# A key norm's reciprocal square root on two engines: square root and reciprocal, or logarithm and exponential

## The chip, the cores and the metric

The kernel runs on one core of a Trainium2 chip. The metric is the time of one execution on the device in microseconds (us), as the median of several runs. Beside the plain runs there is one profiled execution, from which a hardware trace tells what each engine did and when: TensorE (PE, its matmuls, and PEld, its loads of weights), VectorE (DVE), ScalarE (ACT), GpSimd (POOL), SyncE (SP, which issues most transfers), and the DMA engines.

## What is computed

One inference step of a backbone with a single layer, for 512 latent tokens and 128 context tokens, 640 in all, 2,048 channels wide, all in fp32. A layer is an RMS norm with modulation, an input projection `w_in`, a mixer, an output projection, and a gated feed-forward network. Half of the mixer is a bidirectional linear recurrence with 16 heads of 64 channels (RWKV-7), the other half a gMLP with 8 groups. The part that matters here is how the keys of the recurrence are normalised, head by head:

```
kk = heads(k * lp['k_k'])
kk = kk * lax.rsqrt(jnp.maximum(jnp.sum(kk * kk, axis=-1, keepdims=True), 1e-24))
...
y, s_fin = _delta_scan(rh, decay, kd, vh, -kk, kk * heads(a), s0[:, d], reverse=(d == 1))
```

So every key vector of 64 channels is divided by its length. The factor is one number for each token and head, the reciprocal square root of a sum of squares.

## The kernel before

All 640 tokens are held at once, with channels on the 128 partitions and tokens along the free dimension. A projection's 128 output channels for all tokens are a block of 128x640, made as two halves of 320. Since the weights are fp32 and the matmuls take a shorter form of it, each weight piece is split into a high part (ACT, line 172) and a rest (DVE, line 173), and each product is made of three matmuls (lines 194, 195 and 198).

The program has three long stages: the input projection with everything that the mixer needs of each block; the recurrence, with the output projection beside it; and the feed-forward network. The change lies in the first stage.

That stage goes over 43 blocks of `w_in` (list `blocks`, lines 969 to 982). Each block costs 32 small steps of matmuls, which the kernel counts in `wide[0]`; four pieces of 512 input channels make a block, and the split of a piece is issued two pieces ahead (`LEAD`). When a block is complete, `take` (line 996) copies it from PSUM and hands it to a generator that does the rest of its work: `take_r` for a pair of heads' receptance, `take_v` for its values, `take_k` for its keys, `take_gv` and `take_gu` for a gMLP group. The recurrence has eight pairs of heads, and for each pair the order is r, v, k, with one gMLP group or several behind some pairs.

`take_k` (line 562) is by far the longest. For one pair it smooths the keys (lines 572 and 477), squares them and sums the squares over each head with a matmul by a block matrix of ones (`head_sums`, line 519, matmuls at lines 530 and 531), makes the factor (lines 582 to 589), multiplies the keys by it to the tile `nkk` (line 590), and from there makes decay rates (`rates`, matmuls at 605 and 606, tanh at 609; `decays`, line 612), the rows `R` and `X` for the chunk matrices (`rows`, line 629), and the chunk matrices themselves (`chunks`, line 667, matmul at line 677, masked by DVE at lines 688 and 689), for the forward and the backward scan. In its wake come `solve` (line 832), a long chain of small DVE operations (lines 848 and 850), and `merge` (line 862).

How this work is mixed with the projection's matmuls is planned by hand. Every generator yields now and then a number, its estimate of what it has just issued, in a unit of roughly a microsecond; a `Mixer` runs generators until a budget of such units is used up. For the block work the budget comes from a pace: each block has a cost (2.6 for r, 5.1 for v, `KCOST` for k, 12.0 and 5.0 for a gMLP group) and a due time, three blocks ahead:

```python
mixA.add(blocks[b][1](pr), blocks[b][2], wide[0] + 32 * RAW)      # line 1002, RAW = 3
...
for cost, end in self.ends:                                        # line 423, pace()
    need += max(0.0, cost)
    most = max(most, need / max(1, end - wide[0]))
...
mixA.run(f * max(AMIN, 8.0 * mixA.pace()))                         # line 1007, f = 1/4
```

Line 1007 runs four times in each piece of 8 steps, so that one step hands out about as many units as the pace says. `mixS` runs `solve` and `mixM` runs `merge` beside it. The tile framework then puts the instructions of each engine into an order, which need not be that of the program text; in this stage only `in_turn` fixes an order by hand.

On ACT the functions come out of tables, and the trace shows an instruction ACT_TABLE_LOAD where the next function needs another one. In the profile before there are two for each pair: one charged to line 584 (the square root) and one to line 609 (the next tanh).

Of the kernel before, what the change touches and what calls it, by code (L numbers as in the profile page):

```python
# [13 lines left out]
AF = mybir.ActivationFunctionType  # L14
# [10 lines left out]
HALF = T // 2  # L25
# [35 lines left out]
REST = 6  # L61
LATE = 2
OFF = 13
KCOST = 50.0
GORD = (1, 1, 2, 2, 3, 4, 4, 8)
KAP = math.exp(-0.5)
GC0 = math.sqrt(2.0 / math.pi)
# [22 lines left out]
def flow_step(ctx: ExitStack, tc, x_prompt, x_sample, state_rwkv, c, c_ctx, w_mod, b_mod,  # L90
# [4 lines left out]
    V, S, G, TE = nc.vector, nc.scalar, nc.gpsimd, nc.tensor  # L95
# [27 lines left out]
    for h in range(2):  # L123
        s = slice(CH * h, CH * h + CH)
# [9 lines left out]
    for h in range(2):  # L134
        s = slice(CH * h, CH * h + CH)
# [76 lines left out]
    with ExitStack() as ph:  # L212
# [133 lines left out]
        for j in range(4):  # L346
# [5 lines left out]
            for kb in range(4 * j, 4 * j + 4):  # L352
                hf = p0b.tile([P, T], F32, name="hf")
# [208 lines left out]
    def take_k(pr, p):  # L562
# [18 lines left out]
        ssq = bp.tile([P, T], F32, tag="t2", name="ssq", bufs=1)  # L581
        yield from head_sums(sq, lambda ps, s: V.tensor_scalar_max(ssq[:, s], ps, 1e-24))
        yield 1.0
        S.activation(ssq, ssq, AF.Sqrt)
        yield 0.5
        for hf in range(2):
            s = slice(HALF * hf, HALF * hf + HALF)
            V.reciprocal(ssq[:, s], ssq[:, s])
            yield 2.0
        V.scalar_tensor_tensor(out=nkk, in0=nkk, scalar=-1.0, in1=ssq, op0=ALU.mult, op1=ALU.mult)  # L590
        fs = bk.tile([P, T], F32, tag="fs", name="fs", bufs=1)
        yield 0.8
# [378 lines left out]
    def block(col, fn, cost, i):  # L971
        blocks.append((col, lambda pr: fn(pr, i), cost))

    g = 0
    for p in range(NPAIR):
        block(P * p, take_r, 2.6, p)
        block(2 * DA + P * p, take_v, 5.1, p)
        block(DA + P * p, take_k, KCOST, p)
        while g < GORD[p]:
            block(CSH + DA + P * g, take_gv, 12.0, g)  # L980
            block(CSH + P * g, take_gu, 5.0, g)
            g += 1
# [489 lines left out]
    with ExitStack() as ph:  # L1472
# [58 lines left out]
        for hf in range(2):  # L1531
            s = slice(HALF * hf, HALF * hf + HALF)
# [638 lines left out]
```

## Time and profile before

The table gives what matters; stage borders are read from the first and last start of the lines named.

| what | value |
|---|---|
| median of three runs | 3188.06 us (3185.64, 3188.06, 3188.2) |
| profiled execution, its own time | 3182.42 us |
| span of that execution's trace | 3180.6 us |
| mean granted TensorE clock in it | 0.993 of full speed |
| input projection's matmuls (line 194), first and last start | 49.5 and 1062.0 us |
| square root (line 584), first and last start | 195.1 and 901.3 us |
| reciprocal (line 588), first and last start | 195.8 and 905.4 us |
| product with the keys (line 590), first and last start | 200.3 and 907.6 us |

"Busy" is the time in which an engine had an instruction in work; the records of matmuls overlap, since they are pipelined. "Idle before" is the time in which an engine stood still ahead of an instruction, and the name behind `<-` is what ended that wait. A "window" view gives the busy time of each engine in stretches of the span, with the number of instructions in brackets, the granted clock as a share of full speed, and the share of the DMA engines.

### The profile page before, as it was taken

To read this page: it belongs to the slowest core of one execution; us is meant where nothing else is said; L and a number is where in the kernel's file an instruction comes from. 1 tells how busy PE (TensorE), PEld (TensorE's weight loads), DVE (VectorE), ACT (ScalarE), POOL (GpSimd) and SP (SyncE) were. 2 spreads that over 40 slices of the span, in tenths; PEclk is the share of its full clock that TensorE was granted. 3 is DMA by queue.
4 is the path that set the end of the run, shared out by engine and by line. 5 is a ranking of instruction groups with operands and counts; after the bars stand their busy time and mean duration, and the time that the engine had idled before them with its cause. 6 is when DMAs were issued, how large, how long until landed. Compare 5 with 4: busy or idle time off the path is not lost.

```text
span 3180.6 us, 71623 instructions
## 1 busy us (share of the span) xinstructions
PE 3059.6 (96%) x27896; PEld 2844.7 (89%) x27896; DVE 2354.6 (74%) x4119; ACT 1474.4 (46%) x3216; POOL 1238.2 (39%) x1081
## 2 busy tenths in 40 slices
PE   6999999999999999999999999999999999999997
PEld 3788878788878888899999999999999999999997
DVE  4567777667776688767977777777777787888888
ACT  3344544544454444357544444444444454444365
POOL 2001121221122034411456665666656645555542
PEclk9999999999999999999999999999999999999999
DMA  9767786867777688575343434434343364554453
GB/s 371 249 190 201 213 233 175 218 196 203 210 208 202 205 285 275 157 221 155 110 132 107 121 118 127 122 107 127 119 122 119 109 200 150 159 167 123 135 163 123
DMA packets 740436, 550.84 MB, mean 173 GB/s; under 512 B 141056, under 2 KB 673504, under 8 KB 731264
## 3 DMA queue, kind: packets, MB, share of 16 engines
q1 hardware_dynamic: 727136, 532.47, 55.4%
q0 software_dynamic: 10624, 13.23, 1.8%
q8 instruction: 219, 3.59, 0.5%
q14 instruction: 121, 0.99, 0.1%
q10 hardware_dynamic: 2336, 0.57, 0.1%
HBM read 437.79 MB, written 110.95 MB: 173 GB/s over the span
## 4 chain that ended last, share of the span: by engine, by line
PE 45%; DVE 3%; issue 1%; DMA 1%; POOL 1%; ACT 0%; SPq 0%; DVEq 0%; POOLq 0%; ACTq 0%
PE P L1688 15%; PE P L1685 15%; PE P L1686 15%; DVE lo L1466 1%; DMA opd<-d_op 0%; DVE xd L1754 0%; DMA x1d<-d_x 0%; POOL rawd L1594 0%; DVE cd L1944 0%; DMA rawd<-in_w_ffn_down_dram 0%; DVE out L2138 0%; DVE acc L1925 0%; ACT hi L1465 0%; DMA xd<-d_os 0%; POOL t L1594 0%
## 5 line engine op out<-in xcount | busy, mean ns | idle before, releaser
L1685 PE MATMUL P<-xo,hi 128*128 128x320 f32 x2352 | 699.3, 309 | 0.2 <-ACT hi L1465 0.2
L1686 PE MATMUL P<-xo,hi 128*128 128x320 f32 x2352 | 699.1, 309 | 0.0
L1466 DVE TENSOR_TENSOR lo<-raw,hi 128x512 fp32r<-128x512 f32 x526 | 513.0, 981 | 162.3 <-ACT hi L1465 159.8
L1465 ACT CAST hi<-raw 128x512 fp32r<-128x512 f32 x526 | 326.9, 622 | 466.4 <-PE P L1686 384.2
L1688 PE MATMUL P<-xo,lo 128*128 128x320 f32 x2352 | 440.8, 309 | 5.0 <-DVE lo L1466 5.0
L194 PE MATMUL big<-h_hi,hi 128*128 128x320 f32 x1376 | 438.4, 325 | 6.8 <-ACT hi L172 3.9
L1685 PEld LDWEIGHTS P<-xo,hi 128*128 128x128 f32 x2352 | 441.3, 188 | 0.5 <-ACT hi L1465 0.5
L1686 PEld LDWEIGHTS P<-xo,hi 128*128 128x128 f32 x2352 | 441.6, 188 | 0.0
L195 PE MATMUL big<-h_lo,hi 128*128 128x320 f32 x1376 | 423.1, 314 | 0.8 <-DVE h_lo L358 0.7
L1594 POOL TENSOR_TENSOR raw<-raw 128x512 f32<-128x512 f32 x252 | 410.2, 1637 | 10.1 <-DVE lo L1466 1.8
L1688 PEld LDWEIGHTS P<-xo,lo 128*128 128x128 f32 x2352 | 369.0, 188 | 6.0 <-DVE lo L1466 6.0
L1685 PE MATMUL P<-xd,hi 128*128 128x320 f32 x1232 | 367.7, 310 | 5.5 <-ACT hi L1465 2.3
L1686 PE MATMUL P<-xd,hi 128*128 128x320 f32 x1232 | 366.8, 309 | 0.0
L198 PE MATMUL big<-h_hi,lo 128*128 128x320 f32 x1376 | 320.1, 313 | 2.1 <-DVE lo L173 2.1
L194 PEld LDWEIGHTS big<-h_hi,hi 128*128 128x128 f32 x1376 | 261.9, 190 | 57.2 <-issue 25.3
L173 DVE TENSOR_TENSOR lo<-raw,hi 128x512 fp32r<-128x512 f32 x268 | 185.2, 694 | 156.1 <-ACT hi L172 154.4
L1594 POOL TENSOR_TENSOR t<-raw 128x512 f32<-128x512 f32 x84 | 125.1, 1490 | 425.3 <-DMA raw<-in_w_ffn_up_dram 362.0
L1465 ACT CAST hi<-rawd 128x512 fp32r<-128x512 f32 (+1 forms) x288 | 167.0, 585 | 225.3 <-PE P L1686 153.3
L172 ACT CAST hi<-raw 128x512 fp32r<-128x512 f32 x268 | 164.5, 618 | 223.2 <-PE big L195 86.1
L195 PEld LDWEIGHTS big<-h_lo,hi 128*128 128x128 f32 x1376 | 262.0, 190 | 5.8 <-DVE h_lo L358 1.9
L1466 DVE TENSOR_TENSOR lo<-rawd,hi 128x512 fp32r<-128x512 f32 (+1 forms) x288 | 241.3, 844 | 24.6 <-ACT hi L1465 24.3
L1688 PE MATMUL P<-xd,lo 128*128 128x320 f32 x1232 | 236.9, 310 | 7.2 <-DVE lo L1466 7.2
(406 smaller groups left out, 6085.4 us busy)
## 6 DMA issues: line engine op xcount, KB each, us to landing
wt<-in_w_mod_dram SPq DMA_DIRECT2D x96, 1024.0 KB
raw<-in_w_ffn_gate_dram SPq DMA_DIRECT2D x182, 256.0 KB
raw<-in_w_ffn_up_dram SPq DMA_DIRECT2D x182, 256.0 KB
rec<-d_S SPq DMA_DIRECT2D x80, 576.0 KB
raw<-in_w_in_dram SPq DMA_DIRECT2D x172, 256.0 KB
rawd<-in_w_ffn_down_dram SPq DMA_DIRECT2D x128, 256.0 KB
raw<-in_w_out_dram SPq DMA_DIRECT2D x96, 256.0 KB
xd<-d_os SPq DMA_DIRECT2D x66, 320.0 KB
```

What stands on the lines that cost most here:

```text
L172: S.copy(hi, raw)
L173: V.tensor_sub(lo, raw, hi.bitcast(F32))
L194: TE.matmul(halves[hf], hi[:, k, :], h_hi[:, kb, s], start=(kb == 0), stop=False)
L195: TE.matmul(halves[hf], hi[:, k, :], h_lo[:, kb, s], start=False, stop=False)
L198: TE.matmul(halves[hf], lo[:, j - 4 * q, :], h_hi[:, j, s], start=False, stop=(j == KB - 1))
L1465: S.copy(hi[:, 0:nk], raw[:, 0:nk])
L1466: V.tensor_sub(lo[:, 0:nk], raw[:, 0:nk], hi[:, 0:nk].bitcast(F32))
L1594: G.tensor_tensor(out=o[:, 0:nk], in0=p[:, 0:nk], in1=q[:, 0:nk], op=ALU.subtract)
L1685: TE.matmul(ps, hi[:, k, :], xk[:, 0, :], start=q == 0 and k == 0 and not filled, stop=False)
L1686: TE.matmul(ps, hi[:, k, :], xk[:, 1, :], start=False, stop=False)
L1688: TE.matmul(ps, lo[:, k, :], x(i, 4 * q + k)[:, 0, :], start=False, stop=q == nq - 1 and k == nk - 1 and last)
```

## The change

The square root on ACT and the two reciprocals on DVE, each over one half of the tile, are replaced by two ACT operations over the whole tile: the natural logarithm, and an exponential that is given the scale -0.5. Both compute `ssq ** -0.5`. The yields behind them are changed: 0.5, 2.0 and 2.0 go, and one of 1.0 comes. The cost of a key block in the planner goes down by the same 3.5.

```diff
-KCOST = 50.0
+KCOST = 46.5
...
         yield from head_sums(sq, lambda ps, s: V.tensor_scalar_max(ssq[:, s], ps, 1e-24))
         yield 1.0
-        S.activation(ssq, ssq, AF.Sqrt)
-        yield 0.5
-        for hf in range(2):
-            s = slice(HALF * hf, HALF * hf + HALF)
-            V.reciprocal(ssq[:, s], ssq[:, s])
-            yield 2.0
+        S.activation(ssq, ssq, AF.Ln)
+        S.activation(ssq, ssq, AF.Exp, scale=-0.5)
+        yield 1.0
         V.scalar_tensor_tensor(out=nkk, in0=nkk, scalar=-1.0, in1=ssq, op0=ALU.mult, op1=ALU.mult)
```

## The prediction

> **What bounds the kernel now.** I read the page's summary first, then a table of windows, then the waits of TensorE, and last the groups of the lines that change.
>
> ```profile
> span 3180.6 us, 71623 instructions
> PE 3059.6 (96%) x27896; PEld 2844.7 (89%) x27896; DVE 2354.6 (74%) x4119; ACT 1474.4 (46%) x3216; POOL 1238.2 (39%) x1081
> ```
>
> Over the span TensorE is the bound: it stands still for only 3180.6 - 3059.6 = 121.0 us. What VectorE is spared is worth nothing by itself; it pays only where PE waits for it. So I look at the stretch of 30 us that begins with each of the eight pairs' first reciprocal (the starts come from the timeline of line 588), and at what lies between those stretches.
>
> ```profile
> 195.80:225.80 30.00, 29.16 (x216) 24.18 (x214) 26.82 (x41) 17.11 (x38) 4.32 (x8) 1.00 0.58 160
> 299.10:329.10 30.00, 25.80 (x295) 22.23 (x294) 26.61 (x38) 14.02 (x28) 0.53 (x1) 1.00 0.31 82
> 384.70:414.70 30.00, 27.73 (x194) 23.52 (x193) 29.62 (x67) 15.08 (x32) 1.17 (x2) 1.00 0.61 178
> 500.30:530.30 30.00, 30.00 (x282) 25.14 (x281) 28.47 (x43) 15.23 (x33) 1.55 (x3) 1.00 0.60 170
> 595.20:625.20 30.00, 28.15 (x203) 24.42 (x202) 29.51 (x69) 15.27 (x32) 2.26 (x4) 1.00 0.60 181
> 703.90:733.90 30.00, 28.68 (x211) 25.48 (x210) 27.39 (x41) 15.21 (x32) 2.12 (x4) 1.00 0.54 147
> 817.80:847.80 30.00, 26.24 (x387) 22.68 (x387) 27.34 (x42) 14.92 (x30) 0.00 (x0) 1.00 0.59 167
> 902.10:932.10 30.00, 26.20 (x183) 23.30 (x182) 28.77 (x66) 13.97 (x29) 0.40 (x1) 0.94 0.55 169
> sum 240.00, PE 221.95 PEld 190.95 DVE 224.54 ACT 120.83 POOL 12.35; mean PE 27.74 PEld 23.87 DVE 28.07 ACT 15.10 POOL 1.54
> ```
>
> ```profile
> sum 576.20, PE 561.34 PEld 475.76 DVE 351.75 ACT 284.01 POOL 142.29; mean PE 70.17 PEld 59.47 DVE 43.97 ACT 35.50 POOL 17.79
> ```
>
> The columns are busy times of PE, PEld, DVE, ACT and POOL, then the granted clock, the DMA share and GB/s; the last row is the sum over the eight stretches in between, up to 1012 us. Behind each reciprocal DVE is busy 28.07 of 30 us (94%), and PE idles 240.00 - 221.95 = 18.05 us. In between DVE is busy 351.75 of 576.20 us (61%), and PE idles only 14.86 us in more than twice the time. So the first 30 us behind the norm are the place where DVE, and not PE, sets the pace, and the reciprocals stand at its head. ACT is half idle there. Whom PE waits for in the stage (180 to 960 us) agrees:
>
> ```profile
> PE pG L677 <- DVE GA L689: 8.1, 8, 2.4
> PE pG L677 <- DVE mix L848: 3.8, 1, 3.8
> PE pwa L605 <- ACT tha L609: 2.7, 4, 1.3
> PE ptm L180 <- issue: 2.6, 1, 2.6
> ```
>
> (Total us, times, longest.) The largest waits are for DVE's masking of the chunk matrices, a dozen DVE operations behind `nkk`. The tanh, the third, waits in part for DVE as well, whose reads free its tile.
>
> **The change, part by part.** The rows of what goes, what comes, and what has to serve as a price:
>
> ```profile
> L588 DVE RECIPROCAL ssq<-ssq 128x320 f32<-128x320 f32 x16 | 33.7, 2131 | 9.1 <-ACT ssq L584 9.1
> L584 ACT ACTIVATE ssq<-ssq 128x640 f32<-128x640 f32 x8 | 5.9, 740 | 6.0 <-DVE ssq L582 6.0
> L625 ACT ACTIVATE L<-L 128x640 f32<-128x640 f32 x16 | 11.8, 738 | 0.4
> L584 ACT ACT_TABLE_LOAD x8 | 10.3, 1283 | 0.1
> L609 ACT ACT_TABLE_LOAD x8 | 10.3, 1283 | 1.7 <-PE pwa L606 1.6
> ```
>
> *Removed from DVE:* two reciprocals for each pair, 2 x 2.131 = 4.26 us, over eight pairs 34.1 us. They are in no transfer and on no queue but DVE's.
>
> *Exchanged on ACT:* a square root of 0.740 us for a logarithm, and an exponential more. An exponential of this shape takes 0.738 us (line 625). The logarithm is in no row; since the square root and the exponential differ by 2 ns, I take 0.74. ACT gets 8 x 0.74 = 5.9 us more. Queued behind the two are the casts of the weight pieces (line 172) and the copies out of PSUM; ACT is busy 15.10 of 30 us here, and that idle half hides the addition, so I price it at nothing. Without the cover it would be 5.9 us.
>
> *Table loads:* two for each pair now, one for the square root, and one back for the tanh. The exponential of line 625 has none: it shares a table with the tanh. So if the logarithm's table holds no exponential, the load back merely moves from the tanh to the exponential. I take the same two. The bounds are a third load (logarithm, exponential and tanh all apart), 8 x 1.283 = 10.3 us more on ACT, and none at all, 20.5 us less; neither is on the bounding engine while ACT has its idle half. The Trainium skill, "ScalarE: Activation LUTs", section "What ACT_TABLE_LOAD costs", puts a change of tables at about 2.66 us, since a drain of 1.38 us comes ahead of the load. The rows show 0.1 us of idle ahead of all eight loads of line 584 together, so no such drain; by that price the third load would cost ACT an estimated 21.3 us, and my sum would stay as it is, because ACT does not set it.
>
> *The chain from the sum of squares to `nkk`:* square root plus two reciprocals, 0.74 + 4.26 = 5.00 us, become 2 x 0.74 = 1.48 us, 3.52 us shorter (2.24 with a third load in the way).
>
> *The planner.* The yields between the sum and `nkk` fall by 4.5 - 1.0 = 3.5 units, and the cost of a key block by 3.5. This is where most of the gain may be handed back, so it has to be worked out. For a pair whose three blocks follow one another, 2.6 + 5.1 + 50.0 = 57.7 units are due in 96 steps: 0.60 units a step. How long a step is:
>
> ```profile
> L194 PE MATMUL big<-h_hi,hi 128*128 128x320 f32 x1035 | 328.6, 324 | 1.9 <-ACT hi L172 1.9
> ```
>
> One such matmul per step, 1035 in the 780 us from 180 to 960, is 0.754 us a step. So all that follows the norm is handed out 3.5 / 0.60 = 5.8 steps, or 4.39 us, sooner, while DVE is free 4.26 us sooner. As far as that goes, DVE lags behind the plan as much as before. What is left is the thinner plan: 54.2 units instead of 57.7 over the same 96 steps, 6.1% less in each. Of the 28.07 - 4.26 = 23.8 us of other DVE work in a stretch that is 1.45 us that DVE falls less behind. PE can save in each stretch the smaller of 1.45 and its idle time there (30 minus the PE column): 0.84 + 1.45 + 1.45 + 0 + 1.45 + 1.32 + 1.45 + 1.45 = 9.41 us.
>
> The plan is not binding, which keeps this an estimate:
>
> ```profile
> 199.92 0.43 DVE L615 TENSOR_SCALAR sg<-sg 128x640 f32<-128x640 f32 x1
> 200.27 0.81 DVE L590 SCALAR_TENSOR_TENSOR nkk<-nkk,ssq 128x640 f32<-128x640 f32 x1
> ```
>
> Line 615 comes after line 590 in the program text, but runs ahead of it: the order on an engine is arranged once more. What it will be afterwards no row tells.
>
> *Next in line* where a stall goes: TensorE itself. The later stages issue the same instructions, so I expect their lengths to stay.
>
> *Sum:* 9.4 us less. The profiled execution of before took 3182.42 us, 1.82 more than its span; it would be 3173.0. It lies 5.64 us below the median of 3188.06; on the median, **3178.7 us**.
>
> **The rivals.**
>
> *All of the stall goes.* If the planner's part is lost in the rearranging, DVE's lag falls by the whole 4.26 us, which exceeds the idle time of every single stretch (4.20 at most): 18.05 us, and the clock of the last stretch (0.94, 30 x 0.06 = 1.8 us) comes back too: 3168.2. For it: DVE is at 94%, and the longest wait, 3.8 us in the last pair, is one on DVE. Against it: the 4.39 us above.
>
> *Nothing that can be measured.* All of the gain is handed back, or other small waits take its place: 14.86 us of idle time outside the stretches show how many there are. About 3188. A measurement of this kernel can tell some 0.2%, or 6.4 us, from no change, and my 9.4 is not far beyond it.
>
> *Slower: the work is handed out sooner by more than the chain shortens.* PE's chunk matmuls move forward by 4.39 us, but `nkk`, on which they rest, comes only 3.52 us sooner. If PE waits on that chain's latency and not on DVE's queue, each pair loses 0.87 us, together 7.0: 3195.1. With a third load the chain gains 2.24 and the loss is 8 x 2.15 = 17.2 us: 3205.3. It decides as soon as DVE is no longer the fullest engine in the stretch; against it stands that DVE has only 2 us of idle time there, so operations wait for the engine more than for each other.
>
> **How the numbers follow.** The forecast, a gain of 4 to 15 us (3173 to 3184), gets 0.46; about three quarters of it lies beyond 6.4 us, so 0.36 for faster and 0.10 for the same. The whole stall gets 0.12, all faster. No measurable change gets 0.27. Slower gets 0.15, 0.14 of it beyond the bound. That makes 0.48 faster, 0.38 the same, 0.14 slower. The range reaches from the whole stall with its clock (3168) to the slower case without a third load (3195); beyond it lies the third load on a path that turns out to bind, and a rearrangement worse than any of these.
>
> **What the profile of after would show.** Right: no reciprocal, 34 us less DVE time; two ACT operations of about 0.74 us and two table loads for each pair; in the 30 us from each pair's exponential on, DVE nearer 25 than 28 us, and PE idle about 9 us in all instead of 18; the waits of line 677 for lines 689 and 848 about halved; the recurrence and the feed-forward stage as long as before. Wrong: three loads for each pair; PE's idle time in those stretches as large as before (the planner gave it back) or larger, with waits for a DVE that is not full; weight casts of line 172 late behind the new pair on ACT; or a time that moves in the stages behind 1100 us, which I take to stay.

## The result and the profile after

The change made the kernel slower: 3196.86 us as the median of 20 runs (3189.31 to 3206.59), against 3184.63 us for the kernel before in 20 runs (3176.94 to 3189.28). The ratio is 1.0042, 95% interval 1.0035 to 1.005. The prediction was 3178.7 us, with 3195 as the upper end of its range; it was worked out from 3188.06 us, a median of three runs that lies 3.4 us above that of twenty. Of the experiments further down, one run of e4 (3675.97 us, clock 0.751) and one of e14 (5136.78 us, clock 0.711) were slow throughout and are in none of the figures.

The profiled execution took 3192.12 us. First the summary of the changed kernel's page:

```profile
span 3190.3 us, 71610 instructions
PE 3065.2 (96%) x27896; PEld 2847.3 (89%) x27896; DVE 2309.3 (72%) x4103; ACT 1479.0 (46%) x3224; POOL 1240.1 (39%) x1081
```

VectorE is busy 45 us less, of which the reciprocals, whose row is gone, make up 33.7 us; TensorE has the same number of instructions, and the span is 9.7 us longer. Most of that lies in the first stage: its last projection matmul starts at 1070.8 instead of 1062.0 us. The recurrence up to the feed-forward stage takes 480.4 instead of 478.3 us, the feed-forward's larger part 1040.0 instead of 1038.9, the rest 599.0 instead of 601.3. Of the 8.8 us of the first stage, 2.9 are there when the fifth block begins, before any key block: the start of the program differs from execution to execution. Now the stage from the fifth block on, in a windows view (busy PE, PEld, DVE, ACT, POOL, then clock, DMA share, GB/s), of the kernel before:

```profile
152.40:1062.10 909.70, 876.25 (x10628) 753.45 (x10627) 625.73 (x1236) 439.31 (x935) 157.83 (x258) 0.99 0.73 202
```

and of the changed kernel:

```profile
155.30:1070.90 915.60, 879.42 (x10628) 754.18 (x10627) 597.27 (x1220) 443.78 (x943) 157.35 (x258) 0.99 0.73 200
```

The same TensorE instructions, VectorE 28 us less busy, and the stage is 5.9 us longer; TensorE stands idle 36.2 us instead of 33.5, and is busy 3.2 us longer with the same work. Next the 30 us from the exponential of each pair on, in the changed kernel, as the prediction had asked to see them:

```profile
200.47:230.47 30.00, 27.88 (x198) 22.11 (x197) 23.85 (x40) 16.02 (x37) 4.32 (x8) 1.00 0.65 174
306.14:336.14 30.00, 25.67 (x284) 23.13 (x276) 27.45 (x47) 13.53 (x29) 0.53 (x1) 0.94 0.43 114
396.81:426.81 30.00, 26.19 (x164) 21.52 (x163) 24.50 (x53) 13.68 (x32) 6.47 (x10) 0.89 0.73 182
...
sum 240.00, PE 223.15 PEld 186.05 DVE 202.67 ACT 123.96 POOL 38.70; mean PE 27.89 PEld 23.26 DVE 25.33 ACT 15.49 POOL 4.84
```

VectorE fell from 28.07 to 25.33 us, as forecast. TensorE's idle time, forecast at about 9 us, is 240.00 - 223.15 = 16.85 us, where it had been 18.05. The granted clock is 0.94 and 0.89 in the second and third stretch and 0.94 in the fifth (not shown here), where it was 1.00; in the eighth it is 1.00, where it was 0.94. The waits of TensorE in the stage, us in total, times, longest:

```profile
PE pG L674 <- DVE GA L686: 8.8, 7, 2.3
PE big L194 <- ACT hi L172: 2.7, 3, 1.9
```

The wait of line 674 for the masks (line 686 now, 689 before) is 8.8 us where it was 8.1. The single wait of 3.8 us for `mix` (line 848 before) is gone, so the two waits that the prediction wanted halved fell from 11.9 to 8.8 us. And the groups that answer to the prediction's prices:

```profile
L584 ACT ACT_TABLE_LOAD x8 | 10.3, 1283 | 0.1
L584 ACT ACTIVATE ssq<-ssq 128x640 f32<-128x640 f32 x8 | 5.9, 739 | 1.9 <-DVE ssq L582 1.9
L585 ACT ACTIVATE ssq<-ssq 128x640 f32<-128x640 f32 x8 | 5.9, 734 | 0.0
L606 ACT ACT_TABLE_LOAD x4 | 5.1, 1283 | 0.1
L585 ACT ACT_TABLE_LOAD x4 | 5.1, 1283 | 0.1
```

Two loads for each pair, as forecast, and two operations of 0.74 us. But all eight second loads stand between the logarithm and the exponential: in four pairs ahead of the exponential itself, in four ahead of a tanh that was put in between. The timeline of ACT shows one of the former:

```profile
302.50 0.74 ACT L584 ACTIVATE ssq<-ssq 128x640 f32<-128x640 f32 x1 [0.47 <-DVE ssq L582]
304.20 0.62 ACT L172 CAST hi<-raw 128x512 fp32r<-128x512 f32 x1 [0.97 <-PE big L195]
304.84 1.28 ACT L585 ACT_TABLE_LOAD   x1
306.14 0.74 ACT L585 ACTIVATE ssq<-ssq 128x640 f32<-128x640 f32 x1
```

From the start of the logarithm to the end of the exponential go 4.4 us, not 1.48. Over the eight pairs, the time from the end of the sum's second half (line 582) to the end of the product `nkk` falls from a mean of 6.90 to 5.68 us: 1.2 us, where the prediction had 3.5. The first chunk matmul of a pair stands, counted in projection steps from the same point, 28.8 steps behind before and 24.9 now, so 3.9 steps sooner, where the prediction had 5.8.

The Trainium skill, "ScalarE: Activation LUTs", section "Table sets: the hidden batching unit", has one table set with both the exponential and the logarithm, by which no load would stand between them. The four loads of line 585, with only a cast ahead, show that here the table loaded for the logarithm did not serve the exponential. With the set named there the load of 1.283 us would drop out of the chain, by estimate.

### The profile page after: what moved, and what is told of

It is laid out like the page before. It is cut to its first block, busy times and chain, and to the rows that moved or that the text cites. A ratio compares the mean times of both kernels' runs of the same rounds, so it can differ in the third digit from the quotient of the medians.

```text
span 3190.3 us, 71610 instructions
## 1 busy us (share of the span) xinstructions
PE 3065.2 (96%) x27896; PEld 2847.3 (89%) x27896; DVE 2309.3 (72%) x4103; ACT 1479.0 (46%) x3224; POOL 1240.1 (39%) x1081
## 4 chain that ended last, share of the span: by engine, by line
PE 45%; DVE 3%; DMA 2%; issue 1%; POOL 0%; ACT 0%; SPq 0%; DVEq 0%; POOLq 0%; ACTq 0%
PE P L1685 15%; PE P L1682 15%; PE P L1683 15%; DVE lo L1463 1%; DMA opd<-d_op 1%; DMA x1d<-d_x 1%; DVE cd L1941 0%; DVE xd L1751 0%; DVE acc L1922 0%; DVE out L2135 0%; DMA rawd<-in_w_ffn_down_dram 0%; DVE cd L1963 0%; DMA xd<-d_os 0%; SPq L1709 0%; POOL rawd L1591 0%
## 5 line engine op out<-in xcount | busy, mean ns | idle before, releaser
L1463 DVE TENSOR_TENSOR lo<-rawd,hi 128x512 fp32r<-128x512 f32 (+1 forms) x288 | 231.3, 810 | 28.8 <-ACT hi L1462 28.5
```

The source lines that it names most:

```text
L1463: V.tensor_sub(lo[:, 0:nk], raw[:, 0:nk], hi[:, 0:nk].bitcast(F32))
```

## How the runs are split

All runs give a time and a mean granted clock of TensorE. In the 20 runs of the change, those at 0.987 took 3202.38, 3203.77 and 3206.59 us, a mean of 3204.2, and those at 0.991 took 3189.31, 3192.12 and 3192.93 us, a mean of 3191.5. The difference of 12.8 us is 0.004 of 3190. So I split a run's time into time x clock, as what it would take at full clock, and the remainder, as what the clock costs; the means over the runs of a kernel are set against those of the kernel before on the same chip.

The split is a coarse one. A straight line through all 20 runs gives 0.78 us of time for each us counted as lost, and through the runs of the kernel before 0.47 to 0.66, not 1. The 95% intervals of the two columns are 2 to 4 us to either side at full clock and 2 to 5 us for the clock. At a rate of 0.65 a third of the last column would move to the one before it: e1, e6, e13 and e15 would stand at +0.9 to +2.9 us at full clock and e2, e9 and e10 at +7.9 to +11.2, so what is read from the table below holds at that rate as well. "Order" is the share of TensorE's instructions of the first stage that a comparison of the two sequences finds in the same order as in the kernel before.

| kernel | ratio, 95% interval | order | at full clock, us | lost to the clock, us |
|---|---|---|---|---|
| e1 logarithm and exponential, old plan | 1.0019, 1.0008 to 1.003 | 0.97 | +0.9 | +5.6 |
| e2 old operations, new plan | 1.0025, 1.0016 to 1.0033 | 0.82 | +7.4 | +1.5 |
| e3 before, cost 49.5 | 1.0003, 0.9992 to 1.0013 | 0.98 | +2.4 | +0.3 |
| e4 change with one table | 1.0028, 1.0017 to 1.0039 | 0.86 | +5.2 | +5.6 |
| e5 change again | 1.0033, 1.0021 to 1.0045 | 0.87 | +7.1 | +3.6 |
| e6 one operation, old plan | 1.0026, 1.0016 to 1.0035 | 0.97 | +0.3 | +7.5 |
| e7 one operation, new plan | 1.0014, 1.0001 to 1.0026 | 0.84 | +3.1 | +1.3 |
| e8 before and one more exponential | 1.0028, 1.0018 to 1.0037 | 0.91 | +2.9 | +5.5 |
| e9 before, cost 48 | 1.0038, 1.0024 to 1.0052 | 0.86 | +7.2 | +4.9 |
| e10 before, cost 53 | 1.0041, 1.0027 to 1.0054 | 0.42 | +10.2 | +2.7 |
| e11 change, cost 48.5 | 1.0051, 1.0034 to 1.0068 | 0.63 | +9.8 | +6.5 |
| e12 change, cost 44.5 | 1.0017, 1.0007 to 1.0027 | 0.85 | +3.2 | +1.6 |
| e13 one operation, cost 49.5 | 1.0025, 1.0014 to 1.0036 | 0.97 | -0.4 | +8.1 |
| e14 one operation, cost 51 | 1.0036, 1.0023 to 1.0049 | 0.88 | +3.7 | +7.8 |
| e15 logarithm and exponential, cost 49.5 | 1.0017, 1.0007 to 1.0026 | 0.95 | -1.6 | +7.2 |
| e16 before, cost 50.5 | 1.0003, 0.9995 to 1.0012 | 0.96 | +4.4 | -3.2 |
| e17 before, GR stores by GpSimd | 1.0125, 1.0106 to 1.0144 | | +21.9 | +18.2 |
| e18 e1 with GR stores by GpSimd | 1.0147, 1.0132 to 1.0162 | | +20.7 | +25.7 |

## The experiments

The first theory after the result was that of the prediction's third rival, the plan theory: the work behind the norm is handed out some 3 us sooner, and the keys come only 1.2 us sooner. Its rivals: ScalarE's added work, and the order theory, by which any new order of the instructions costs something.

**Operations and plan apart (e1, e2), a mere nudge (e3), one table (e4).** e4 leaves the key norm out: its factor is a constant.

```diff
 # e1, against the change
-KCOST = 46.5
+KCOST = 50.0
         S.activation(ssq, ssq, AF.Ln)
+        yield 0.5
         S.activation(ssq, ssq, AF.Exp, scale=-0.5)
-        yield 1.0
+        yield 2.0
+        yield 2.0
 # e2: sqrt and reciprocals as before, KCOST = 46.5, behind them only yield 1.0
 # e3, against before: KCOST = 49.5
 # e4, against the change
-        S.activation(ssq, ssq, AF.Ln)
-        S.activation(ssq, ssq, AF.Exp, scale=-0.5)
+        S.activation(ssq, ssq, AF.Tanh)
+        S.activation(ssq, ssq, AF.Exp, scale=-2.3)
```

> Logarithm and exponential, but the yields and the key block's cost of before (0.5, 2.0, 2.0 and 50.0). Plan theory (the change is slower because the work behind the norm is handed out some 4 steps, about 3 us, sooner for each pair, while the keys come only 1.2 us sooner): nothing is handed out sooner, the keys still come over 1 us sooner and VectorE is spared 34 us, so it is as fast as before or faster, ratio 0.997 to 1.000. ScalarE theory (the table load and the second operation stand in the way of casts and tanh): as slow as the change, 1.003 to 1.005. Order theory (any new order of the instructions moves the time by some tenths of a per cent): anything from 0.997 to 1.005.

> Square root and reciprocals as before, but the yields and the cost of the change (one yield of 1.0, 46.5). Plan theory: the work is handed out sooner and the keys come no sooner at all, so slower than the change, ratio 1.004 to 1.010. ScalarE theory: as before, 0.999 to 1.001. Order theory: anything from 0.997 to 1.005.

> The kernel of before with a key block's cost of 49.5 instead of 50.0 and nothing else: a new order with no other reason to be faster or slower. Plan theory and ScalarE theory: within 0.2% of before. Order theory: off by 0.2% to 0.5% to either side.

> The change with a tanh in the logarithm's place and -2.3 as the exponential's scale, so that the key norm's factor is a constant and not the norm, but all three functions share one table: no load of tables for any pair, and the keys come 1.3 us or more sooner than in the change. ScalarE theory: the loss goes, ratio 0.998 to 1.000. Plan theory: the keys are now about 3 us sooner than before and the work 3 us, so most of the loss goes as well, 0.999 to 1.002. Order theory: anything from 0.997 to 1.005.

Measured: 1.0019, 1.0025, 1.0003 and 1.0028. The plan alone, with the old operations, costs 0.25%, somewhat less than the plan theory had. But the operations alone, with the old plan, cost 0.19% where that theory had none. Without table loads the loss is 0.28%, within the interval of the change's 0.33% (e5). The ScalarE theory had no loss for e2, and 0.998 to 1.000 for e4. No single theory holds; the nudge, which leaves 98% of the order, does nothing.

**Less work, and more (e5 to e8).** e5 is the change once more. e6 and e7 make the factor with one ScalarE function, so that the keys come 4 us sooner with no work added anywhere; e8 adds an exponential to the kernel before.

```diff
 # e6, against before (e7: with KCOST = 46.5 and one yield 1.0)
-        S.activation(ssq, ssq, AF.Sqrt)
+        S.activation(ssq, ssq, AF.Abs_reciprocal_sqrt)
         yield 0.5
-        for hf in range(2):
-            ...
-            V.reciprocal(ssq[:, s], ssq[:, s])
-            yield 2.0
+        yield 2.0
+        yield 2.0
 # e8, against before
         S.activation(ssq, ssq, AF.Sqrt)
+        S.activation(sq, ssq, AF.Exp, scale=-0.5)
```

> The change itself once more, on the chip of the three that follow, so that their granted clocks can be compared. All theories: ratio 1.003 to 1.005.

> One ScalarE function makes the whole factor (the reciprocal square root of the absolute value), with the yields and the cost of before: VectorE is spared its 34 us, ScalarE has as many operations and table loads as before, the keys come 4.3 us sooner, and nothing is handed out sooner. The reason of the prediction (VectorE sets the pace behind the norm): the idle time there goes, 12 to 18 us, ratio 0.994 to 0.997. ScalarE theory (the loss comes from the second operation and from the load of tables between the two): no loss here, 0.995 to 1.000. Cover theory (VectorE's time behind the norm is not what TensorE waits for; the waits come from the order in which the chunk work is issued): 0.999 to 1.002.

> The same single function, with the yields and the cost of the change (1.0 and 46.5). Plan theory: the work is handed out 3 us sooner and the keys come 4.3 us sooner, so the loss of the plan does not show, ratio within 0.001 of the run before it. If the plan costs its 0.0025 whatever the chain, this is 0.0025 above the run before it.

> The kernel of before with one exponential of 128x640 more behind the square root, whose output nobody reads: 5.9 us more of ScalarE, the load of the tanh's table moved ahead of it, the chain to the keys and the plan untouched. ScalarE theory: 1.001 to 1.003. Plan theory: 0.999 to 1.001.

Measured: 1.0033, 1.0026, 1.0014 and 1.0028. e6 is the run that fells the prediction's reason: all of VectorE's 34 us spared, the chain 4.4 us shorter (2.52 instead of 6.90 us), ScalarE as before, TensorE's order 97% that of before, and the kernel is slower by 0.26%. So VectorE's time at the norm was not what TensorE waited for. It was also slower by as much as e8, which spares nothing and adds 5.9 us to ScalarE; work saved and work added cost the same. But e8 does not leave the chain untouched, as was expected of it: the reciprocals write over the tile that the exponential reads, so they wait for it, 17.5 us in all, and the chain takes 9.78 instead of 6.90 us. Its 1.0028 lies in the range of the ScalarE theory, and does not tell ScalarE's time from the longer chain. e7 is not 0.0025 above e6 but, if anything, below it: the plan does not have a price of its own that adds to others. The plan theory had the two within 0.001 of each other, which the intervals allow.

**Other costs in the plan, for no reason (e9 to e12).** Only `KCOST` differs: 48.0 and 53.0 in the kernel before, 48.5 and 44.5 in the change.

> The kernel of before with a key block's cost of 48.0 instead of 50.0. Order theory (any new order costs 0.1 to 0.4%, whatever its reason, since each lays the stalls of TensorE elsewhere): ratio 1.001 to 1.004. Systematic theory (the loss of the change comes from its own operations and plan, the small change of a cost does nothing): 0.999 to 1.001.

> The kernel of before with a key block's cost of 53.0. Order theory: 1.001 to 1.004. Systematic theory: 0.999 to 1.001; the plan theory, by which a thicker plan makes VectorE lag more and TensorE wait more, 1.001 to 1.003.

> The change with a key block's cost of 48.5 instead of 46.5. Order theory: off from the change by 0.1 to 0.3% to either side, so anything from 1.000 to 1.006, and other than the next run. Systematic theory: as the change, 1.003 to 1.005.

> The change with a key block's cost of 44.5. Order theory: anything from 1.000 to 1.006, and other than the run before it. Systematic theory: as the change, 1.003 to 1.005.

Measured: 1.0038, 1.0041, 1.0051 and 1.0017. This decides against the plan theory. The kernel before, with nothing changed but the planner's figure, and in either direction, loses as much as the change lost; the change, with another figure, ranges from 1.0017 to 1.0051. e9 hands out at a slightly lower pace, and its first chunk matmul stands later in the chain, not sooner (31.1 steps instead of 28.8), so the plan theory has nothing for its 0.38%. That it is the order which costs is what remains, and is not shown by itself: the share of the order that is kept does not rank the losses (e9 0.86 and 0.38%, e12 0.85 and 0.17%). The waits of TensorE in e9 show that other stalls have come up:

```profile
PE pG L677 <- DVE GA L689: 11.5, 8, 2.5
PE pW L711 <- ACT XT L703: 4.6, 6, 1.8
PE pG L677 <- ACT gend L626: 4.3, 2, 3.3
```

**Neighbours with nearly the order of before (e13 to e16).** `KCOST` 49.5 and 51.0 with the single function, 49.5 with e1's operations, 50.5 in the kernel before.

> The single function with a key block's cost of 49.5 (the yields of before). Order theory: scatters, 0.998 to 1.004, and off from the run with 50.0 (1.0026) by more than 0.001. Theory that the operations cost clock: 1.002 to 1.004, with a mean granted clock under 0.990.

> The single function with a key block's cost of 51.0. Order theory: scatters, 0.998 to 1.004, and off from the other two. Theory that the operations cost clock: 1.002 to 1.004, with a mean granted clock under 0.990.

> Logarithm and exponential with the yields of before and a key block's cost of 49.5. Order theory: scatters, 0.998 to 1.005. Theory that the operations cost clock: 1.001 to 1.004, with a mean granted clock under 0.990.

> The kernel of before with a key block's cost of 50.5. Order theory: 1.000 to 1.004, as its order comes out near to that of before or not. Theory that the operations cost clock: 0.999 to 1.001, with the granted clock of before.

Measured: 1.0025, 1.0036, 1.0017 and 1.0003. These do not scatter as the order theory had it, and all four lie where the theory that the operations cost clock had them. The four kernels with 95% or more of the order of before and without the reciprocals (e1, e6, e13, e15) lie at 1.0017 to 1.0026; the two with them (e3, e16) at 1.0003. At full clock the four are within 1.6 us of before; the clock costs them 5.6 to 8.1 us more. So near the order of before there is a second cost that goes with sparing the reciprocals, and it is lost clock. In other orders kernels that keep the reciprocals lose as much of it (e8 5.5 us, e9 4.9 us).

Where e6 loses it can be read in windows of one and two times 3.41 us:

```profile
398.28:401.70 3.42, 1.88 (x13) 0.73 (x5) 3.36 (x6) 1.84 (x4) 1.17 (x2) 1.00 1.05 262
401.70:408.52 6.82, 6.20 (x30) 3.91 (x30) 6.32 (x12) 3.45 (x7) 2.46 (x4) 0.50 0.65 150
```

After a window with TensorE busy only 1.88 of 3.42 us, the clock is 0.50 for two windows. The profiles of e1, e6, e13 and e15 all have such a stretch of half clock at 401 to 406 us, and those of before, e3 and e16 have none there. In e6 TensorE's longest waits in that first window are 0.87 us for a tanh (line 607) and 0.67 us for `X` (line 655); before has a wait of 1.3 us for a tanh there and no half clock behind it. Three of the four (e1, e6, e15) have another such stretch at 630 us. There e6's TensorE waits 2.86 us ahead of a transpose of line 695 (697 before), and VectorE's timeline tells why:

```profile
625.76 0.29 DVE L686 TENSOR_TENSOR GR<-pG,mask 128x128 f32<-128x128 f32 x1 [1.37 <-DMA d_S<-GR]
...
627.78 0.29 DVE L686 TENSOR_TENSOR GR<-pG,mask 128x128 f32<-128x128 f32 x1 [1.40 <-DMA d_S<-GR]
```

VectorE is not late with work here. It stands still, because the masked tile `GR` has two buffers, and their stores to HBM (line 692 before) have not landed. The same holds of the other two: in e1 VectorE stands still for 2.48 and 0.98 us there, in e15 for 4.07 us, while TensorE waits 3.5 and 4.1 us. In the kernel before VectorE waits for these stores as well:

```profile
L688 DVE TENSOR_TENSOR GR<-pG,mask 128x256 f32<-128x256 f32 (+1 forms) x96 | 36.1, 376 | 24.8 <-DMA d_S<-GR 11.5 <-PE pG L677 7.0 <-PE pblk L885 3.2
```

and in e6 for 14.8 us:

```profile
L686 DVE TENSOR_TENSOR GR<-pG,mask 128x256 f32<-128x256 f32 (+1 forms) x96 | 36.3, 378 | 26.1 <-DMA d_S<-GR 14.8 <-PE pG L675 9.9
```

These rows do not explain the change. VectorE waits 8.7 us for the stores in it, less than before. And such a wait costs TensorE only where TensorE stands still at the same time. Laid over each other, the two timelines have 0.0 us of that in the kernel before, 0.2 in the change, 1.6 in e6, 2.2 in e1 and 3.8 in e15. TensorE's waits for the masks in the kernel before look otherwise. Here VectorE, and then TensorE, in one of them:

```profile
723.70 0.42 DVE L688 TENSOR_TENSOR GR<-pG,mask 128x256 f32<-128x256 f32 x1
724.15 0.43 DVE L689 TENSOR_TENSOR GA<-pG,mask 64x256 f32<-64x256 f32 x1
724.61 0.42 DVE L688 TENSOR_TENSOR GR<-pG,mask 128x256 f32<-128x256 f32 x1
724.95 0.41 DVE L689 TENSOR_TENSOR GA<-pG,mask 64x256 f32<-64x256 f32 x1
725.50 0.71 PE L677 MATMUL pG<-R,X 64*128 64x128 f32 x8 [0.93 <-DVE GA L689]
```

VectorE works on the masks without a break, and TensorE goes on when the last is done. In all eleven waits for these masks (lines 677 and 697, 8.1 + 1.5 us between 180 and 960 us) VectorE is at work for 8.3 of the 9.6 us, 6.3 of them on the masks themselves.

**The stores of GR on another queue (e17, e18).**

```diff
-  nc.sync.dma_start(d_S[p, :, d, c0:c1, F_G + CH * h:F_G + CH * h + CH], GR[:, 0:c1 - c0, :])
+  BQ.dma_start(d_S[p, :, d, c0:c1, F_G + CH * h:F_G + CH * h + CH], GR[:, 0:c1 - c0, :])
```

> The kernel of before, with the stores of the masked tile GR issued by GpSimd and no longer by SyncE. Ring theory (the stores wait in SyncE's queue, VectorE waits for them, TensorE for VectorE): VectorE's wait for DMA d_S<-GR falls below 6 us from 11.5, ratio 0.997 to 1.000. Order theory: 1.000 to 1.004. If the store's own latency is the limit: the wait stays over 10 us, 1.000 to 1.003.

> Logarithm and exponential with the old plan, with the same move of the stores. Ring theory: the stalls of 2 to 4 us are gone, the spared VectorE time shows at last, ratio 0.994 to 0.999 and below the run before it. Theory that the operations cost clock whatever stands behind them: 0.002 above the run before it. If the store's own latency is the limit: as without the move, 1.001 to 1.003.

Measured: 1.0125 and 1.0147, both far above the ranges that were given. The wait became longer, not shorter; in e17:

```profile
L688 DVE TENSOR_TENSOR GR<-pG,mask 128x256 f32<-128x256 f32 (+1 forms) x96 | 36.3, 378 | 71.6 <-DMA d_S<-GR 49.1 <-PE pG L677 16.0 <-PE big L198 1.3
```

```profile
PE pG L677 <- DVE GA L689: 26.4, 13, 3.6
```

VectorE waits 49.1 us for the stores instead of 11.5, TensorE 26.4 us instead of 8.1 for the masks, and the kernel takes 1.25% longer. Of VectorE's 49.1 us, 21.2 fall on idle time of TensorE. That shows that late stores can cost TensorE time. How much of the 1.25% is theirs stays open, since GpSimd also issues the transfers of `solve` and `merge` (lines 838, 857, 867 and 924), which now share its queue with the stores. Nor does it show that quicker stores or a third buffer would win back the 0.2%; a third buffer was not tried. e18 lies 0.0022 above e17, as the theory that the operations cost clock had it, and the clock makes up all of it (25.7 instead of 18.2 us), though the two intervals overlap.

No kernel of the eighteen beat the kernel before; e3 and e16 equal it.

## Why the prediction was wrong

*What bounds the stage.* The view was right, and the reading of it was not. VectorE was 94% busy in the 30 us behind the norm, and TensorE idled there for 18 us; from this the prediction took VectorE's queue for the cause. The step that failed is "PE can save in each stretch the smaller of 1.45 and its idle time there". e6 took 34 us off that queue and 4.4 us off the chain at nearly the same order, and gained nothing at full clock (+0.3 us); in the change VectorE fell to 25.33 us in each stretch and TensorE's idle time only from 18.05 to 16.85 us. What the traces show in its place: TensorE waits for particular operations, the masks, and in those waits VectorE was at work on the masks themselves for 6.3 of 9.6 us. With the reciprocals gone the same waits (8.8 + 0.9 us in the change, 9.2 + 3.6 in e6) are no shorter. That an engine is 94% busy in a stretch did not tell that the operation TensorE waits for was late because of it.

*The prices on the engines* were right: the reciprocals' 33.7 us are gone from VectorE, each of the two operations takes about 0.74 us, and each pair has two loads. The other 11 us by which VectorE is less busy are not the change's doing as far as is known: the profiles of before and e10, with the same operations, differ by 17 us (2354.6 and 2337.5). ScalarE's second operation, priced at nothing, cost nothing that can be measured: e1, which has it, and e6, which has not, are equal within their intervals (1.0019 and 1.0026).

*The chain.* "3.52 us shorter" was 1.2 us. The prediction moved the load back from the tanh to the exponential, but left its 1.28 us out of the chain, although in that place it lies on it. A cast or a tanh slipping in between took the rest. This was a mis-sized term, and not the cause of the loss: with a chain 4.4 us shorter (e6) the loss is there as well.

*The planner.* That the gain would be handed back by the plan was the right suspicion for a wrong reason. The work came 3.9 steps sooner and not 5.8. "What it will be afterwards no row tells" was said of the order, and then a rearrangement got no term in the sum; it stands only among what lies beyond the range. It has a price: e2, e9 and e10 change no operation and lose 0.25 to 0.41%, most of it at full clock (7.2 to 10.2 us). In the change the loss at full clock is the larger part, 7.1 us beside 3.6 us of clock (e5), though the latter is no larger than its interval.

*The rivals.* The slower rival, at 3195.1 us, came nearest in time, and the measurement lies just above it. That is luck: it had 7.0 us of loss upon a start that was 3.4 us too high, and the loss is 12.2 us. Its mechanism fell: it made e1 equal to before or faster (1.0019), e2 slower by 0.4% or more (1.0025), and it has nothing for e9 (1.0038), where the work is handed out later.

*The clock.* The prediction gave it 1.8 us in one stretch, as something to win back. By the split above it is worth 25 (e16) to 57 us (e18) over a whole execution, and it differs by 5 to 8 us between kernels whose work at full clock is equal within the intervals.

What stays open: why the four kernels near the order of before lose clock. The profiles point to two stretches of half clock that before lacks: one at 401 to 406 us, in e6 behind waits of under 1 us each, and in three of the four one at 630 us, where VectorE is seen waiting for the stores of `GR`. That these make up all of the 5.6 to 8.1 us is argued, not shown; each kernel has one profile, and that of before is one of its better executions (clock 0.993). e7 and e12, also without reciprocals but in other orders, lose only 1.3 and 1.6 us of clock, which speaks against a property of the operations alone; their intervals, 4.5 and 3.3 us to either side, do not exclude it. Nor is it shown what in an order costs the 3 to 10 us at full clock, and so the cause of the larger part of the change's loss stays open.

## What to carry to other kernels

When an engine is busy all through a stretch in which TensorE idles, look at what that engine does during the waits themselves, and just ahead of the instructions that release TensorE, before counting time spared elsewhere as a gain: here it was at work on those very instructions, and in a few waits of other kernels it stood still for a store. In a kernel whose order is arranged anew at every edit, run a few edits that should do nothing: here a planner's figure 4 to 6% away cost as much as the change did, and the kernel before sat at the bottom of that scatter. Compare kernels at full clock and in lost clock apart, since a stall can cost more in clock than in idle time.

## What the runs showed of the hardware

The clock falls by halves, in stretches that are multiples of 3.41 us. It needs no long pause of TensorE: in e6 a window of 3.42 us with 1.54 us of idle time in it was followed by 6.82 us at 0.50, and in the profile of before 3.41 us at half clock from 660.28 us on followed a window in which TensorE stood still for 0.87 us, the end of a stall of 1.19 us, and had mostly matmuls of 32x32 and 64x64 to do; whether their size counts is not shown. So the 1.54 us of idle time in e6 cost up to 3.4 us more (6.82 x 0.50). The Trainium skill, "TensorE: Matmul & The Clock Gate", section "Part 1: The HAM clock gate (the "warmup" mystery)", has the halves and a window of about 3.4 us, and lets the clock fall after an idle window; here windows that were about half busy sufficed. The stretches differ between executions of one program: the two profiles of the change (after and e5) share four places, and only e5 has half clock at 894 us. The runs of the change range over 0.987 to 0.992.

A store of 128 KB issued by GpSimd took 4.5 us from issue to landing in e17, as a median, and 3.6 us in e18; the profile gives no such figure for the same store issued by SyncE.
